# VectorE and ScalarE in written order behind the output products, weights split five units ahead

## The chip, the cores and the metric

The kernel runs on one core of one Trainium2 chip. The metric is device microseconds (us) of one execution; the time of a kernel is the median of its runs. About 0.2% (some 5 us) is what a measurement of this kernel can tell from no change.

## What is computed

Two stacks in a chain, for 256 positions and width 1024, all in fp32: two hybrid layers (retention, gated linear attention and forgetting attention side by side, then a convolved gated feed-forward part), and four layers with one mixer each (mLSTM, sliding window, HGRN2, differential attention) and a SwiGLU part. Every norm is modulated by columns that come from a product of a conditioning vector with large matrices ("ada"). Cut to what matters here:

```python
def hybrid_layer(...):                      # twice
    mod = c_act @ w_ada + b_ada
    h = modulate(rms_norm(x, norm1_g), shift1, scale1)
    ...                                     # three branches of h @ w_in
    mixed = jnp.sum(gates * y_br, axis=2) @ w_o
    x = x + gate1 * mixed
    h2 = modulate(rms_norm(x, norm2_g), shift2, scale2)
    u, g = jnp.split(h2 @ w_up, 2, axis=-1)
    u = causal_dwconv(u, w_conv, b_conv)    # three taps
    x = x + gate2 * ((jax.nn.silu(u) * g) @ w_down)

def layer(x, mixer):                        # four times: DeepNorm form
    ...                                     # x = layer_norm(ALPHA * x + (1 + gate) * mixer(modulate(x)))
def swiglu(h, w_in, w_out):
    gu = h @ w_in
    return (jax.nn.silu(gu[..., :FFN_HIDDEN]) * gu[..., FFN_HIDDEN:]) @ w_out
```

## The kernel before

**Products.** Each fp32 product is made of split parts: a weight and an activation are each held as a high part and a low rest, and a 128x128 block costs three matmuls (high by high, high by low, low by high; L497 to L499 where the output has features on partitions). Weights come in **units** of 128x1024, 689 of them, that is eight blocks. `load_unit` fetches a unit by DMA, casts it to the high part on ScalarE (the **cast**, tile h, L465) and subtracts on VectorE (the **low**, tile l, L466); `blocks` calls it when a unit's first block is about to be used. The h and l buffers are five deep each (pool ph). A product tile gathers eight blocks (22 in the products named down and fo) into one of four PSUM buffers (dps). In the transposed products the first four tiles that follow a norm run as one group on the unnormed activations (the early tiles, y, L765 and L766), and the norm's factors are applied behind it (fix, L777 to L781); four more tiles (mps) run on the normed ones, and single tiles follow.

**Stages.** By name: wo, up and down are the output product and the feed-forward part of the two hybrid layers; ml_w, sw_w, hg_w and df_w are the output products of the four mixers, fi and fo their feed-forward parts, and sw_in, hg_*, df_* the first products of the next mixers. At the end of an output product the residual tiles Z0 to Z7 (or X0 to X7) are formed; sums of their squares go through TensorE (stat), a chain of small VectorE instructions on 128x2 tiles makes the inverse root (`moments`, L721 to L734, with L671 to L679 in `rsqrt_short`), TensorE spreads it over the partitions (L743), ScalarE copies that (L746), and the tiles follow (L1380 to L1389).

**In the hybrid feed-forward part** tiles come in pairs: the even one gets its first tap on ScalarE (Identity, L859 from dps), two taps on VectorE (L1243, L1245) and silu (L859 from t); the odd one multiplies (L1251), and the product is split (L486 on ScalarE, L487 on VectorE). SwiGLU has silu, product and split alone.

**The order.** The program is written down instruction by instruction, and a scheduler then decides the order on every engine from its own costs; only pieces under `issue_after` are tied to others. The ada pieces (288 of 512 KB, one VectorE sum each, L415) are put in by `pump` at rates per stage (RATES): so many a product tile.

## Time and profile before

| | |
|---|---|
| median of 3 runs | 2322.12 us (2321.53 to 2323.61) |
| the profiled execution: its own time | 2321.35 us |
| its span in the trace | 2319.0 us |
| TensorE busy / weight loads | 2203.2 / 2115.6 us |
| VectorE busy | 1819.6 us |
| ScalarE busy | 1264.3 us |
| GpSimd busy | 106.8 us |
| mean granted TensorE clock | 0.979 of full speed |

TensorE is busy in 95% of the span. What is left is some 116 us at which it stands still, the start and the tail among them. Starts of the stages that the text speaks of, in us: up0 301 to 428, down0 to 491, the second hybrid layer's mixer to 751, wo1 to 774, up1 to 901, down1 to 965, ml_w 1067 to 1091, fi0 1091, sw_in 1295, sw_w 1348, fi1 1392, fo1 1531, hg 1596 to 1764, fi2 1764, df 1965 to 2103, fi3 2103, fo3 2240.

### The profile page before, as it was taken

Reading aid. Unit: us, or ns where it says so; the run is one execution under the profiler, and the core shown is the slowest. Engines: PE = TensorE matmul, PEld = TensorE weight load, DVE = VectorE, ACT = ScalarE, POOL = GpSimd, SP = SyncE. Lnnn points to the kernel's source line nnn. Section 1 sums busy time; section 2 is a strip of 40 time slices with the busy share of each in tenths; the row PEclk is TensorE's granted clock in tenths of the full one; section 3 lists DMA queues with packets and bytes.
Section 4 is the critical chain, followed back from the end, with each engine's and each line's share of the span. In section 5 each row is a group of like instructions: output and inputs, shape, how many; then the busy total and the mean of one; then the engine's idle time right before and its main releaser. Section 6 shows DMA issues by size and latency. Waiting matters only on the chain.

```text
span 2319.0 us, 46070 instructions
## 1 busy us (share of the span) xinstructions
PE 2203.2 (95%) x18071; PEld 2115.6 (91%) x18071; DVE 1819.6 (78%) x3465; ACT 1264.3 (55%) x2452; POOL 106.8 (5%) x280
## 2 busy tenths in 40 slices
PE   6999999999999999989899998999988999988997
PEld 5899999997999999979899888999878999878997
DVE  8879897988778878947878868688668778968655
ACT  3545465555454654545644676445755544766543
POOL 0011000002010000021000000000010000030000
PEclk9999999999999999989999998999998999999999
DMA  9659756978677568935789426787444788434751
GB/s 368 241 184 356 261 193 220 360 254 281 229 268 240 173 227 283 380 128 181 246 272 312 144 92 199 229 286 240 156 151 150 237 266 288 164 119 147 244 182 37
DMA packets 144938, 521.14 MB, mean 225 GB/s; under 512 B 16208, under 2 KB 18512, under 8 KB 144720
## 3 DMA queue, kind: packets, MB, share of 16 engines
q1 hardware_dynamic: 144432, 518.03, 65.5%
q8 instruction: 141, 2.31, 0.4%
q14 instruction: 77, 0.63, 0.1%
q10 hardware_dynamic: 288, 0.16, 0.0%
HBM read 517.08 MB, written 1.05 MB: 223 GB/s over the span
## 4 chain that ended last, share of the span: by engine, by line
PE 42%; issue 26%; DVE 3%; ACT 3%; POOL 2%; DMA 1%; ACTq 0%; POOLq 0%; DVEq 0%
PE dps L497 12%; PE dps L498 12%; PE dps L499 11%; POOL nr L634 1%; PE dps L506 1%; PE dps L505 1%; PE dps L504 1%; ACT t L859 1%; ACT h L465 1%; DVE l L466 1%; DMA w<-in_ada_dram 1%; PE mps L497 0%; PE mps L498 0%; PE mps L499 0%; PE mps L1674 0%
## 5 line engine op out<-in xcount | busy, mean ns | idle before, releaser
L497 PE MATMUL dps<-t,h 128*128 128x256 f32 (+1 forms) x4776 | 1358.3, 285 | 1.5 <-ACT t L791 0.7
L498 PE MATMUL dps<-t,h 128*128 128x256 f32 (+1 forms) x4776 | 1349.8, 283 | 2.3 <-DVE t L487 1.3
L499 PE MATMUL dps<-t,l 128*128 128x256 f32 (+1 forms) x4776 | 1347.2, 282 | 1.7 <-DVE l L466 1.7
L465 ACT CAST h<-w 128x1024 fp32r<-128x1024 f32 x689 | 719.8, 1052 | 539.0 <-PE dps L498 281.8
L466 DVE TENSOR_TENSOR l<-w,h 128x1024 fp32r<-128x1024 f32 x689 | 838.4, 1221 | 211.3 <-ACT h L465 208.4
L497 PEld LDWEIGHTS dps<-t,h 128*128 128x128 f32 x4776 | 904.6, 190 | 6.4 <-issue 1.9
L499 PEld LDWEIGHTS dps<-t,l 128*128 128x128 f32 x4776 | 905.6, 190 | 4.0 <-DVE l L466 2.1
L498 PEld LDWEIGHTS dps<-t,h 128*128 128x128 f32 x4776 | 904.2, 189 | 4.9 <-DVE t L487 2.3
L415 DVE SCALAR_TENSOR_TENSOR junk<-w,cb 128x1024 bf16<-128x1024 f32 x288 | 351.6, 1221 | 97.1 <-DMA w<-in_ada_dram 90.6
L486 ACT CAST t<-t 128x256 fp32r<-128x256 f32 x172 | 69.3, 406 | 125.8 <-DVE t L1419 75.6
L504 PE MATMUL dps<-h,t 128*128 128x512 f32 (+1 forms) x288 | 105.2, 374 | 8.3 <-ACT t L1388 6.3
L505 PE MATMUL dps<-l,t 128*128 128x512 f32 (+1 forms) x288 | 105.8, 371 | 1.6 <-DVE l L466 1.6
L506 PE MATMUL dps<-h,t 128*128 128x512 f32 (+1 forms) x288 | 104.3, 371 | 0.0
L816 POOL TENSOR_SCALAR nr<-nr 128x2 f32<-128x2 f32 (+2 forms) x22 | 13.3, 606 | 1592.5 <-ACT junk L859 1562.4
L487 DVE TENSOR_TENSOR t<-t,t 128x256 fp32r<-128x256 f32 x172 | 71.1, 419 | 8.7 <-ACT t L486 8.7
L504 PEld LDWEIGHTS dps<-h,t 128*128 128x128 f32 x288 | 56.3, 196 | 17.6 <-ACT t L1388 7.1
L765 ACT ACTIVATE t<-Z,c 128x256 fp32r<-128x256 f32 x56 | 28.5, 508 | 74.9 <-DVE Z L1364 74.9
L505 PEld LDWEIGHTS dps<-l,t 128*128 128x128 f32 x288 | 56.4, 196 | 10.8 <-DVE l L466 2.8
L506 PEld LDWEIGHTS dps<-h,t 128*128 128x128 f32 x288 | 55.8, 196 | 8.1 <-DVE t L1389 0.2
L497 PE MATMUL mps<-t,h 128*128 128x256 f32 x192 | 47.6, 308 | 15.1 <-ACT t L1388 13.6
L498 PE MATMUL mps<-t,h 128*128 128x256 f32 x192 | 55.0, 298 | 0.1
L499 PE MATMUL mps<-t,l 128*128 128x256 f32 x192 | 54.3, 295 | 0.0
(383 smaller groups left out, 2021.1 us busy)
## 6 DMA issues: line engine op xcount, KB each, us to landing
w<-in_w_dram SPq DMA_DIRECT2D x689, 512.0 KB, 4.5
w<-in_ada_dram SPq DMA_DIRECT2D x288, 512.0 KB, 5.1
t<-in_c_dram SPq DMA_DIRECT2D x4, 256.0 KB, 4.2
X<-in_x_dram SPq DMA_DIRECT2D x8, 128.0 KB, 3.8
v<-in_ret_dram SPq DMA_DIRECT2D x2, 512.0 KB, 9.0
out_dram<-X SPq DMA_DIRECT2D x8, 128.0 KB, 2.0
cols<-in_cols_dram SPq DMA_DIRECT2D x1, 737.0 KB, 6.8
const<-in_const_dram SPq DMA_DIRECT2D x1, 387.0 KB, 7.8
```

The source lines that it names most:

```text
L415: self.nc.vector.scalar_tensor_tensor(out=self.junk, in0=w, scalar=0.5, in1=self.cb, op0=ALU.mult, op1=ALU.mult, accum_out=self.mod[l][:, ...
L465: nc.scalar.copy(h[:, q:e], raw[:, q:e]).ins,
L466: nc.vector.tensor_tensor(out=low[:, q:e], in0=raw[:, q:e], in1=h[:, q:e].bitcast(F32), op=ALU.subtract).ins]
L486: nc.scalar.copy(t[:, 0], src)
L487: nc.vector.tensor_tensor(out=t[:, 1], in0=src, in1=t[:, 0].bitcast(F32), op=ALU.subtract)
L497: mm(pt, lhsT=h, rhs=x[:, 0], start=first, stop=False)
L498: mm(pt, lhsT=h, rhs=x[:, 1], start=False, stop=False)
L499: self.last_mm = mm(pt, lhsT=low, rhs=x[:, 0], start=False, stop=last).ins
L504: mm(pt, lhsT=x[:, 0, sl], rhs=h, start=first, stop=False)
L505: mm(pt, lhsT=x[:, 0, sl], rhs=low, start=False, stop=False)
L506: self.last_mm = mm(pt, lhsT=x[:, 1, sl], rhs=h, start=False, stop=last).ins
L765: self.nc.scalar.activation(out=h, in_=z, func=AF.Copy, scale=a)
```

## The change

From wo0 on to the end of down1, and from ml_w on to the end of the program, VectorE and ScalarE get a hand-written order (`manual_schedule`): their instructions stand in the order in which the program writes them. TensorE, GpSimd and the DMA queue are still ordered by the scheduler. Nothing closes the order at the next first products: `free_order` is called at the end of down1 and at the end, and the flag `ending` is set but read nowhere. So the second hybrid layer's mixer and the mixers swa, hgrn and diff are inside.

Inside it, `blocks` issues the split of unit u+5 at the first block of unit u; h and l get six buffers. The low half of an activation's split is held until the next weight unit has been split (or another point of release). A product tile's ada pieces are handed out block by block, and the rates change. `residual` loses its tie to the last tile. Counts of instructions stay the same, but for one table load less on ScalarE. Line numbers of the new kernel: cast L472, low L473, ada L422, activation split L521 and L522, Identity and silu L903, taps L1288 and L1290, product L1296, residual L1392 and L1412, early L806 to L808, moments L762 to L775 with L711 to L719, spread L784 and copy L787, fix L820 to L824, tile L1428 to L1438.

```diff
-RATES = dict(... up=0.1, down=3, fi=0.2, fo=2.5, ... fi0=0.5, ...)
+RATES = dict(... up=0.3, down=1.5, fi=0.36, fo=1.5, ... fi0=0.6, ...)
-        self.ph = ctx.enter_context(tc.tile_pool(name="ph", bufs=5))
+        self.ph = ctx.enter_context(tc.tile_pool(name="ph", bufs=6))
...
     def blocks(self, n):
-        if self.cunit is None or self.cunit[0] != u:
-            self.cunit = (u, self.load_unit(u * UNIT))
+        while max(self.ready, default=-1) < min(u + self.ahead, len(self.units) - 1):
+            i = max(self.ready, default=-1) + 1
+            self.ready[i] = self.load_unit(*self.units[i])
+            self.release()
+    def hold(self, piece):
+        if self.order is None:
+            piece()
+        else:
+            self.held.append(piece)
+    def ordered(self):
+        if self.order is None:
+            self.order = ExitStack()
+            self.order.enter_context(self.tc.manual_schedule(engines={mybir.EngineType.DVE, mybir.EngineType.Activation}))
+            self.ahead = AHEAD
...
         if scale is None:
             nc.scalar.copy(t[:, 0], src)
-            nc.vector.tensor_tensor(out=t[:, 1], in0=src, in1=t[:, 0].bitcast(F32), op=ALU.subtract)
+            self.hold(lambda: nc.vector.tensor_tensor(out=t[:, 1], in0=src, in1=t[:, 0].bitcast(F32), op=ALU.subtract))
...
+            if self.order is not None:
+                self.pump(pump / kt)
-        self.pump(pump)
+        if self.order is None:
+            self.pump(pump)
...
+        self.ordered()
         n2 = self.rms_begin(l, 3, "n2")
...
+        if last:
+            self.free_order()
+        self.ending = True
...
+            self.ordered()
             hx = self.residual_norm(("ml_w", "sw_w", "hg_w", "df_w")[i], ys, i, 0, None if last else nxt)
```

**VectorE in the product up0, before.** Two pairs of tiles; l is the low of a weight unit, the tiles t with numbers are activations.

```order
L466 TENSOR_TENSOR l<-w,h 128x1024
L1243 SCALAR_TENSOR_TENSOR t_4253<-dps,cols,t_4253 128x255
L1245 SCALAR_TENSOR_TENSOR t_4253<-dps,cols,t_4253 128x254
L466 TENSOR_TENSOR l<-w,h 128x1024
L1251 TENSOR_TENSOR t_4253<-t_4253,dps 128x256
L487 TENSOR_TENSOR t_4290<-t_4253,t_4290 128x256
L466 TENSOR_TENSOR l<-w,h 128x1024
L1243 SCALAR_TENSOR_TENSOR t_4324<-dps,cols,t_4324 128x255
```

**The same place after.**

```order
L1296 TENSOR_TENSOR t_4578<-t_4578,dps 128x256
L473 TENSOR_TENSOR l<-w,h 128x1024
L522 TENSOR_TENSOR t_4618<-t_4578,t_4618 128x256
L1288 SCALAR_TENSOR_TENSOR t_4652<-dps,cols,t_4652 128x255
L1290 SCALAR_TENSOR_TENSOR t_4652<-dps,cols,t_4652 128x254
L473 TENSOR_TENSOR l<-w,h 128x1024
L1296 TENSOR_TENSOR t_4652<-t_4652,dps 128x256
```

The low half of the product's split (L522) now stands behind the next unit's low, and ahead of the taps.

**ScalarE in up0, before.** L859 from dps is the first tap, L859 from t the silu.

```order
L465 CAST h<-w 128x1024
L859 ACTIVATE t_4253<-dps,cols 128x256
L465 CAST h<-w 128x1024
L859 ACTIVATE t_4253<-t_4253 128x256
L486 CAST t_4290<-t_4253 128x256
L465 CAST h<-w 128x1024
```

**The same place after.**

```order
L472 CAST h<-w 128x1024
L903 ACTIVATE t_4288<-dps,cols 128x256
L903 ACTIVATE t_4288<-t_4288 128x256
L472 CAST h<-w 128x1024
L521 CAST t_4325<-t_4288 128x256
L472 CAST h<-w 128x1024
```

The second cast of a pair stood ahead of the silu and stands behind it now.

**VectorE at the start of fi1, before:** the end of the chain of small instructions (nr) and the first instructions behind the spread (L778 on).

```order
L466 TENSOR_TENSOR l<-w,h 128x1024
L673 TENSOR_TENSOR nr<-nr 128x2
L415 SCALAR_TENSOR_TENSOR junk,mod_128<-w,cb 128x1024
L674 TENSOR_TENSOR nr<-nr 128x2
L466 TENSOR_TENSOR l<-w,h 128x1024
L675 SCALAR_TENSOR_TENSOR nr<-nr 128x2
L415 SCALAR_TENSOR_TENSOR junk,mod_128<-w,cb 128x1024
L676 SCALAR_TENSOR_TENSOR nr<-nr 128x2
L677 TENSOR_TENSOR nr<-nr 128x2
L678 SCALAR_TENSOR_TENSOR nr<-nr 128x2
L679 SCALAR_TENSOR_TENSOR nr<-nr 128x2
L734 TENSOR_TENSOR nr<-nr 128x2
```

**The same place after.**

```order
L714 TENSOR_TENSOR nr<-nr 128x2
L715 SCALAR_TENSOR_TENSOR nr<-nr 128x2
L716 SCALAR_TENSOR_TENSOR nr<-nr 128x2
L717 TENSOR_TENSOR nr<-nr 128x2
L718 SCALAR_TENSOR_TENSOR nr<-nr 128x2
L719 SCALAR_TENSOR_TENSOR nr<-nr 128x2
L775 TENSOR_TENSOR nr<-nr 128x2
L473 TENSOR_TENSOR l<-w,h 128x1024 x3
L821 TENSOR_TENSOR t_17249<-dps,t_17210 128x256
```

The chain now stands in one piece, and three lows of weight units stand between it and the first fix (L821).

**VectorE at the end of the output product sw_w, before:** the last residual tiles (Z_120 and Z_121 are Z6 and Z7).

```order
L1344 SCALAR_TENSOR_TENSOR Z_118<-dps,mod_127,X_90 128x256
L1344 SCALAR_TENSOR_TENSOR Z_119<-dps,mod_127,X_91 128x256
L1364 TENSOR_TENSOR Z_118<-Z_118,t_16792 128x256
L1364 TENSOR_TENSOR Z_119<-Z_119,t_16792 128x256
L713 TENSOR_TENSOR t_16791<-t_16791,Z_118 128x256
L766 SCALAR_TENSOR_TENSOR t_16990<-Z_118,c_16777,t_16990 128x256
```

**The same place after.**

```order
L1392 SCALAR_TENSOR_TENSOR Z_118<-dps,mod_127,X_90 128x256
L1412 TENSOR_TENSOR Z_118<-Z_118,t_16764 128x256
L749 TENSOR_TENSOR t_16763<-t_16763,Z_118 128x256
L808 SCALAR_TENSOR_TENSOR t_16965<-Z_118,c_16749,t_16965 128x256
L752 TENSOR_TENSOR t_16762<-t_16762,t_16968 128x256
L473 TENSOR_TENSOR l<-w,h 128x1024
L1392 SCALAR_TENSOR_TENSOR Z_119<-dps,mod_127,X_91 128x256
```

Two residual tiles ran interleaved; now one tile is finished, with a weight unit's low behind it, before the next begins.

## Rows read from the trace of the kernel before

**Rows 1.** The page, busy time of each engine.

```profile
PE 2203.2 (95%) x18071; PEld 2115.6 (91%) x18071; DVE 1819.6 (78%) x3465; ACT 1264.3 (55%) x2452; POOL 106.8 (5%) x280
```

**Rows 2.** Groups by line, up0's steady stretch (317 to 428.4): count, busy us, mean ns, idle before.

```profile
L466 DVE TENSOR_TENSOR l<-w,h 128x1024 fp32r<-128x1024 f32 x39 | 47.6, 1219 | 6.7 <-ACT h L465 6.7
L415 DVE SCALAR_TENSOR_TENSOR junk<-w,cb 128x1024 bf16<-128x1024 f32 x12 | 14.6, 1219 | 4.0 <-DMA w<-in_ada_dram 4.0
```

**Rows 3.** Timeline of VectorE in up0: start, length (us), line, idle before and releaser.

```profile
360.92 0.48 DVE L1243 SCALAR_TENSOR_TENSOR t<-dps,cols,t 128x255 f32<-128x255 f32 x1
361.43 0.48 DVE L1245 SCALAR_TENSOR_TENSOR t<-dps,cols,t 128x254 f32<-128x254 f32 x1
361.83 1.22 DVE L466 TENSOR_TENSOR l<-w,h 128x1024 fp32r<-128x1024 f32 x1
362.96 0.42 DVE L1251 TENSOR_TENSOR t<-t,dps 128x256 f32<-128x256 f32 x1
363.85 0.42 DVE L487 TENSOR_TENSOR t<-t,t 128x256 fp32r<-128x256 f32 x1 [0.47 <-ACT t L486]
364.80 1.23 DVE L466 TENSOR_TENSOR l<-w,h 128x1024 fp32r<-128x1024 f32 x1 [0.53 <-ACT h L465]
365.95 0.48 DVE L1243 SCALAR_TENSOR_TENSOR t<-dps,cols,t 128x255 f32<-128x255 f32 x1
```

**Rows 4.** Timeline of ScalarE in the same stretch.

```profile
360.56 1.06 ACT L465 CAST h<-w 128x1024 fp32r<-128x1024 f32 x1 [0.36 <-PE dps L498]
362.01 0.42 ACT L859 ACTIVATE t<-t 128x256 f32<-128x256 f32 x1 [0.39 <-DVE t L1245]
363.41 0.41 ACT L486 CAST t<-t 128x256 fp32r<-128x256 f32 x1 [0.99 <-DVE t L1251]
363.73 1.05 ACT L465 CAST h<-w 128x1024 fp32r<-128x1024 f32 x1
```

**Rows 5.** Windows: stretch, length, busy PE, PEld, DVE, ACT, POOL, granted clock, DMA share, GB/s.

```profile
317.00:428.40 111.40, 111.40 (x949) 111.36 (x947) 96.49 (x166) 68.25 (x112) 0.00 (x0) 1.00 0.68 231
428.40:490.70 62.30, 62.30 (x531) 62.30 (x531) 58.84 (x92) 29.87 (x46) 0.00 (x0) 1.00 0.98 374
1423.00:1531.40 108.40, 108.40 (x922) 108.31 (x920) 76.40 (x121) 59.65 (x96) 0.00 (x0) 1.00 0.72 233
490.70:751.00 260.30, 254.99 (x1886) 236.98 (x1884) 206.35 (x365) 132.91 (x247) 26.85 (x48) 0.99 0.71 243
1295.10:1391.90 96.80, 94.52 (x700) 81.33 (x699) 71.85 (x223) 73.05 (x204) 0.00 (x0) 0.96 0.26 83
1596.20:1764.30 168.10, 152.56 (x1834) 137.74 (x1833) 126.65 (x269) 108.11 (x302) 14.76 (x48) 0.98 0.47 152
1964.90:2102.70 137.80, 124.17 (x978) 116.09 (x977) 107.80 (x290) 94.08 (x247) 27.58 (x96) 0.94 0.41 135
1391.90:1423.00 31.10, 22.78 (x160) 22.27 (x159) 24.49 (x60) 13.62 (x27) 0.00 (x0) 0.78 0.60 203
2067.90:2080.00 12.10, 9.30 (x75) 8.62 (x73) 3.78 (x5) 7.88 (x27) 8.30 (x33) 1.00 0.49 163
```

**Rows 6.** Timeline from sw_w's end (1391.9) to the restart in fi1, cut.

```profile
1393.82 0.48 DVE L1344 SCALAR_TENSOR_TENSOR Z<-dps,mod,X 128x256 f32<-128x256 f32 x1
1395.34 0.42 DVE L1364 TENSOR_TENSOR Z<-Z,t 128x256 f32<-128x256 f32 x1
...
1409.92 2.08 PE L743 MATMUL mps<-const,nr 128*128 128x128 f32 x8 [4.92 <-DVE nr L679]
1412.03 0.59 ACT L746 COPY t<-mps 128x512 f32<-128x512 f32 x1 [5.97 <-PE mps L743]
1412.65 0.42 DVE L778 TENSOR_TENSOR t<-dps,t 128x256 f32<-128x256 f32 x1 [2.59 <-ACT t L746]
...
1415.39 1.01 PE L497 MATMUL mps<-t,h 128*128 128x256 f32 x3 [3.40 <-ACT t L1388]
```

**Rows 7.** Groups by line, whole span: the spread's matmuls on TensorE, with their waits.

```profile
L743 PE MATMUL mps<-const,nr 128*128 128x128 f32 x80 | 15.0, 340 | 22.3 <-DVE nr L679 18.9 <-DVE nr L664 3.3
```

More of the change, by code (lines that the diff above doesn't have):

```diff
@@ L28 @@
 LATE = True
+AHEAD = 5
 SUMS, KNOWN = 5, 21
@@ L189, in pack_ada @@
     return out
-RATES = dict(rv0=0, rk0=0, rq0=0.05, gk0=0, gg0=1, rg0=2, mg0=0.75, up=0.1, down=3, fi=0.2, fo=2.5, wo=0.0, ml_w=0.0,
+RATES = dict(rv0=0, rk0=0, rq0=0.05, gk0=0, gg0=1, rg0=2, mg0=0.75, up=0.3, down=1.5, fi=0.36, fo=1.5, wo=0.0, ml_w=0.0,
              sw_w=0.0, hg_w=0.0, df_w=0.0, br=1.0, sw_in=0.0, df_kq=0.0, df_v0=2.0, df_v1=0.0, hg_v=1.5, ml_v=3.0,
-             fq=3.0, fk=3.0, fv=3.0, gv=3.0, rv=3.0, gk=1.5, hg_qf1=0.2, s1=1.25, fi0=0.5, hg_g=0.6, ml_o=0.6,
+             fq=3.0, fk=3.0, fv=3.0, gv=3.0, rv=3.0, gk=1.5, hg_qf1=0.2, s1=1.25, fi0=0.6, hg_g=0.6, ml_o=0.6,
              gv1=1.25, fv1=4, wo0=0.1, df_kq1=0.1, ml_v1=4)
@@ L310, in __init__ @@
         self.specs, _ = dense_specs()
+        self.units, self.ready, self.ahead, self.order = [], {}, 0, None
+        for s in self.specs:
+            s["first"] = len(self.units)
+            self.units += [(s, lo) for lo in range(0, s["cols"], UNIT)]
         self.si = 0
+        self.held = []
+        self.ending = False
         self.bg = list(range(len(ADA_ORDER)))
@@ L449, in begin, with load_unit @@
         self.si += 1
-        self.cur, self.cpos, self.cunit = s, 0, None
+        self.cur, self.cpos = s, 0
         return s
-    def load_unit(self, lo):
-        nc, s = self.nc, self.cur
+    def load_unit(self, s, lo):
+        nc = self.nc
         hi = min(s["cols"], lo + UNIT)
@@ L470, in blocks @@
     def blocks(self, n):
-        pos = self.cpos
-        u, r = divmod(pos, UNIT)
-        if self.cunit is None or self.cunit[0] != u:
-            self.cunit = (u, self.load_unit(u * UNIT))
-        h, low = self.cunit[1]
+        u, r = divmod(self.cpos, UNIT)
+        u += self.cur["first"]
+        while max(self.ready, default=-1) < min(u + self.ahead, len(self.units) - 1):
+            i = max(self.ready, default=-1) + 1
+            self.ready[i] = self.load_unit(*self.units[i])
+            self.release()
+        for i in [i for i in self.ready if i < u and i + 8 < max(self.ready)]:
+            del self.ready[i]
+        h, low = self.ready[u]
         assert r + n <= UNIT
@@ L479, in blocks, with release, free_order @@
         return h[:, r:r + n], low[:, r:r + n]
+    def hold(self, piece):
[3 more added lines that the diff above has]
+            self.held.append(piece)
+    def release(self):
+        while self.held:
+            self.held.pop(0)()
+    def ordered(self):
[3 more added lines that the diff above has]
+            self.ahead = AHEAD
+    def free_order(self):
+        if self.order is not None:
+            self.release()
+            self.order.close()
+            self.order, self.ahead = None, 0
     def split(self, src, scale=None):
@@ L547, in dense_tile @@
                 self.step(self.mid)
-        self.pump(pump)
+            if self.order is not None:
+                self.pump(pump / kt)
+        if self.order is None:
+            self.pump(pump)
         return pt
@@ L589, in dense_T @@
                 norm["later"].pop(0)()
+        self.release()
         return xs
@@ L707, in stat @@
         self.act(out=two(sq), in_=z, func=AF.Square)
+        if f and sums["centred"]:
+            nc.vector.tensor_tensor(out=two(acc[1]), in0=sums["first"] if f == 1 else two(acc[1]), in1=z, op=ALU.add)
+        self.release()
         if f:
@@ L711, in stat @@
             sums["first"] = z
-        if f and sums["centred"]:
-            nc.vector.tensor_tensor(out=two(acc[1]), in0=sums["first"] if f == 1 else two(acc[1]), in1=z, op=ALU.add)
     def moments(self, st, centred, eps):
@@ L765, in early @@
         self.nc.scalar.activation(out=h, in_=z, func=AF.Copy, scale=a)
-        self.nc.vector.scalar_tensor_tensor(out=low, in0=z, scalar=a, in1=h.bitcast(F32),
-                                            op0=ALU.mult, op1=ALU.subtract)
         self.nc.scalar.copy(y[:, :, S:S + 2], ab[:, :, f, :])
+        self.hold(lambda: self.nc.vector.scalar_tensor_tensor(
+            out=low, in0=z, scalar=a, in1=h.bitcast(F32), op0=ALU.mult, op1=ALU.subtract))
+        if f == 7:
+            self.release()
         return y
@@ L790, in modulated @@
         t = self.t2([128, 2, S], F32R)
+        self.release()
         nc.scalar.activation(out=t[:, 0], in_=u, func=AF.Identity, bias=B[:, f:f + 1])
-        nc.vector.scalar_tensor_tensor(out=t[:, 1], in0=u, scalar=B[:, f:f + 1], in1=t[:, 0].bitcast(F32),
-                                       op0=ALU.add, op1=ALU.subtract)
+        self.hold(lambda: nc.vector.scalar_tensor_tensor(
+            out=t[:, 1], in0=u, scalar=B[:, f:f + 1], in1=t[:, 0].bitcast(F32), op0=ALU.add, op1=ALU.subtract))
         return t
@@ L1386, in tile @@
             u = self.t1()
+            self.release()
             self.act(out=two(u), in_=z[f], func=AF.Identity, scale=cA[:, f:f + 1], bias=cB[:, f:f + 1])
-            ready[0] = nc.scalar.copy(t[:, 0], u).ins
-            nc.vector.tensor_tensor(out=t[:, 1], in0=u, in1=t[:, 0].bitcast(F32), op=ALU.subtract)
+            nc.scalar.copy(t[:, 0], u)
+            self.hold(lambda: nc.vector.tensor_tensor(out=t[:, 1], in0=u, in1=t[:, 0].bitcast(F32), op=ALU.subtract))
             return t
-        ready = {}
         def residual(f):
-            with self.tc.issue_after(ready[0]):
+            if True:
                 self.act(out=two(self.X[f]), in_=z[f], func=AF.Identity, scale=aG[:, f:f + 1], bias=aB[:, f:f + 1])
@@ L2028, in finish @@
     def finish(self):
+        self.free_order()
         for f in range(8):
```

4 lines of the change are left out of this document (3 added, 1 removed).

## The prediction, made before the changed kernel was run

> **What bounds the kernel now.** I read the busy times first [rows 1]: TensorE 2203.2 of 2319.0 us, so it is the bound and can give back 116 us at the most. VectorE at 78% and ScalarE at 55% look free, but these are means over stages. I took the stretches next [rows 5]. In up0 VectorE is busy 96.49 of 111.40 us and ScalarE 68.25, TensorE all of it at full clock: VectorE and ScalarE together have 164.7 us of work in 111.4, so 53 us of it must overlap, and the order decides whether it can. In fi1 the sum is 136.1 of 108.4. Then I went down to single instructions in up0 [rows 3, 4], to the start of fi1 [rows 6], and to the spread's waits over the whole span [rows 7].
>
> **The pair loop in up, the main term.** One pair of tiles is a loop through both engines, since each instruction hands on to the next. Before, from start to start [rows 3, 4]: product L1251 at 362.96, activation cast 363.41 (0.45), weight cast 363.73 (0.32), low 364.80 (1.07), first tap 365.95 (1.15), second tap (0.51, from 360.92 to 361.43), low (0.40), product (1.13, 361.83 to 362.96). That sums to 5.03, which is the distance of the two first taps shown, 360.92 and 365.95. TensorE needs longer: 39 units in 111.40 us [rows 2, 5], 2.86 a tile, 5.71 a pair. So the loop hides, with 0.7 us to spare, and ada sums fit in here and there.
>
> Three things get into that loop by the new order. The held low half (L522) comes between the low and the taps: one 0.42 instruction [rows 3], about 0.38 back to back. The second weight cast stands behind the silu, so the second tap must end, the silu run and the cast follow: 0.58 (361.43 to 362.01) for silu to begin, 0.32 until the cast can (as for the activation cast, 363.41 to 363.73), then 1.07 to the low and 1.13 to the product, where before the low followed the tap after 0.40 because its cast was done. The new loop: 0.45 + 0.32 + 1.07 + 1.13 + 0.38 + 0.51 + 0.58 + 0.32 + 1.07 + 1.13 = 6.96 us. The Identity is hidden beside the low. The split ahead doesn't help: it moves which unit is cast, not where in the queue the cast stands.
>
> Single tiles in up are 36 of 44, or 18 pairs: 18 x (6.96 - 5.71) = 22.5 us. Up to ten ada sums in up0 and nine in up1 now stand between a low and the next evacuation, on the loop, at 1.14 to 1.22 each [rows 2]: about 11 us. Of these 33.5 the four PSUM buffers let TensorE run ahead by up to three tiles, 8.6 us, but what isn't lost there is partly lost at down's first tile, which needs the last hidden tile near its end; I take off 8. So **+26 a time, +52 for up0 and up1**. Ends for both together: +20 if the ada sums find holes and the buffers and down's slack absorb more than half of the rest, +67 if nothing is absorbed.
>
> **The start of a feed-forward part.** In fi1 before, the last residual tile is finished at 1395.76, 3.9 us behind sw_w's end, the spread begins at 1409.92, and the normed product restarts at 1415.39, 23.5 us behind [rows 6]. The chain of small instructions in between has weight lows and ada sums in every joint. After, it runs in one piece: some 14 instructions of about 0.2, so 3 us. Against that, the residual tiles come later. One written tile is residual and shift (0.8 us together, as two instructions like those of rows 3), early cast and square on ScalarE (0.9 with the hand-over), weight cast 1.05, low 1.14: about 4.0 a tile for tiles 4 to 7, where TensorE needs 2.86, and about 2.2 each for tiles 0 to 3. From the group's end, 12.4 us ahead of the stage's end, that is 8.8 + 1.2 + 3 x 4.0 + 0.9 = 22.9, so Z7 is done 10.5 us behind the end, 6.6 later than now. Sum and chain give the spread at some 15.5 (now 18.0). Then the three lows: the third waits for a cast that stands behind the spread's copy, so 2.7 us to the copy's end, 1.05 and 1.22, and from there 2.7 to the restart as now (1412.65 to 1415.39): 23 to 26. Over fi0 to fi3 I take +2 each, **+8**, ends -20 and +30. For the two ups, whose start is short now, the written tile loop costs some 5 each, **+11** with the clock behind it, ends 0 and +20.
>
> **The mixers.** They fall under the written order too. The sum of both engines beyond the stretch's length, which would be the loss if nothing overlapped [rows 5]: second hybrid mixer 206.35 + 132.91 - 260.3 = 79, sliding window 48, HGRN2 67, differential 64, together 258. Between these ends two rows have a worked loop: in up 33.5 of 53 come out, six tenths; in fi the loop without taps is product, activation cast, weight cast, silu, weight cast, low, 0.45 + 0.32 + 0.96 + 0.35 + 1.07 + 1.13 = 4.3, or 5.4 with an ada sum, under 5.71, so none of 28 does. The mixers have several heads side by side, but rotary chains and exponentials are written head by head; they are nearer to fi in load and to up in the length of a chain. I take 15%, **+40**, ends 0 and +130.
>
> **Edits with one answer.** down and fo have fewer ada sums: VectorE is at 58.84 of 62.30 in down0 and TensorE has no gap there [rows 5], so at most a microsecond or two in fo: **-4**. fi's own steady part: 0. One table load less, the sixth buffer and the released `residual`: 0, as TensorE waits for none of them.
>
> **Sum**, against the profiled execution's own 2321.35: +52 + 8 + 11 + 40 - 4 = +107, so 2428.4; the median is 0.8 higher, so **2429**. All low ends together give 2318, all high ends 2565; half-way to each, since they won't all fall together, 2374 to 2497.
>
> **Rivals.**
> 1. *Faster: the chain in one piece wins.* TensorE waits 18.9 us for the chain at six norms [rows 7], and behind such a wait the granted clock is low: 0.78 over the first 31.1 us of fi1, with 22.78 busy [rows 5]. If up's loop hid (the lead of five units and the buffers swallowing it) and the residual tiles kept TensorE's pace, the 18.9 would go, and about half as much again at the clock: 2321 - 30 = 2290. It decides at the written tile loop being under 2.86 and the pair loop under 5.71. Against it: the sums above, worked out from distances seen between the same instructions. Chance 0.20, of which 0.03 end within 0.2%.
> 2. *The up loop hides, the rest stays:* an order of instructions that overlaps better than I read, or slack in the buffers. Then 2429 - 52, with a few us, 2380. Chance 0.11.
> 3. *The mixers serialise as much as up does,* half of their 258: 2429 + 90 = 2520. For it: VectorE and ScalarE take turns on each item. Against it: several heads in flight. Chance 0.10.
> 4. *TensorE's clock falls in up.* In the slow stretch TensorE would wait about 1.3 to 1.9 us in each pair. In 2067.9 to 2080 it was busy 9.30 of 12.1 us, with waits of 1 to 2 us, and the clock stayed at 1.00 [rows 5]; so I expect full clock at a share of 5.71 in 7.6. [...] Chance 0.05.
> That the change doesn't do what its few words say is so in one point already: the written order doesn't end at the next first products, which is in the mixers' term. If it were closed there, that term would go and the time be 2389, still slower.
>
> **How the numbers follow.** The forecast has 0.54, and the rivals 0.20, 0.11, 0.10 and 0.05. Predicted is the forecast's 2429. Its own range, 2374 to 2497, holds rivals 2 and 4 too; to leave out no more than 2 in 10 I go down to 2300, into the upper part of rival 1, and up to 2530 for rival 3. Within 0.2% is about what a measurement of this kernel can tell from no change. Faster by more: 0.17, from rival 1. Within: 0.03. Slower: the forecast and rivals 2 to 4, 0.80.
>
> **What would show it.** In up0 after: the product L1296 every 7.0 us, 7.6 where an ada sum stands in between, with TensorE waiting for VectorE on a PSUM buffer, up0 at about 150 us in place of 127, VectorE's share of it lower, and the lows waiting for casts. In fi1: the spread about 15 us behind the output product's end and the restart at 23 to 26; L743's waits shorter, the group's matmuls waiting for the last early tiles instead. In sliding window, HGRN2 and differential attention some 5 to 15 us more each, with TensorE waiting on both engines in turn. I would be wrong in the main term if the pair distance in up stays under 5.75, in the boundaries if the restart comes before 20, in the mixers if their stretches don't grow.

## The result, and the profile after

The changed kernel takes 2603.46 us (2601.61 to 2606.02) beside 2322.83: a ratio of 1.121, interval 1.119 to 1.123. It is slower, as forecast, but by 281 us and not by 107, and lies above the range that was given (2300 to 2530).

The busy times of the page after, to be laid beside [rows 1]:

```profile
PE 2292.1 (88%) x18071; PEld 2168.1 (83%) x18071; DVE 1860.8 (72%) x3465; ACT 1260.4 (48%) x2451; POOL 107.3 (4%) x280
```

The same work in a longer span: VectorE's share falls from 78 to 72%, ScalarE's from 55 to 48%, TensorE's from 95 to 88%; the engines wait for each other. TensorE's busy time grew as well, by 89 us for the same number of matmuls, at a mean granted clock of 0.946 (before 0.979). The spans are 2319.0 and 2599.8 us. By stage, from a stage's first matmul to the next one's, in us ("mixer" with the output product behind it, and the second hybrid mixer without wo1):

```
                     before   after   forecast     closed   closed, silu, old rates
up0 + up1             253.8   337.0     +63         336.8     274.4
second hybrid mixer   260.3   292.0  )              272.4     273.6
sliding window         96.8   138.4  )  +40          98.5     104.1
HGRN2                 168.1   200.5  )  in all      179.5     176.8
differential          137.7   199.5  )              164.5     145.5
fi0 to fi3            553.2   573.7     +8          574.7     573.5
down and fo           399.0   405.9     -4          407.0     402.1
```

A forecast of +63 is the prediction's +52 and +11. "Closed" is the run with the order closed at the next first products, and the last column takes two more causes away; both are below. The up products lost 83 us (63 forecast with their starts), the four mixers 168 (40 forecast), fi0 to fi3 21 (8 forecast, for their starts). The stretches of after that answer to [rows 5] (a part of up0, the second hybrid mixer, sliding window, HGRN2, differential; columns as there):

```profile
349.00:400.00 51.00, 42.45 (x333) 40.65 (x332) 31.59 (x49) 21.20 (x34) 0.00 (x0) 0.98 0.53 176
533.10:825.10 292.00, 264.25 (x1885) 241.49 (x1884) 208.99 (x359) 129.85 (x249) 28.18 (x48) 0.98 0.65 222
1417.80:1556.20 138.40, 105.75 (x699) 86.80 (x698) 77.12 (x221) 71.38 (x197) 0.00 (x0) 0.80 0.22 73
1764.80:1965.30 200.50, 162.79 (x1833) 145.06 (x1832) 133.25 (x272) 106.98 (x294) 13.00 (x48) 0.91 0.42 141
2178.50:2377.90 199.40, 145.46 (x977) 131.00 (x976) 126.47 (x309) 94.26 (x245) 28.06 (x96) 0.83 0.36 125
```

In sliding window VectorE's and ScalarE's busy times add up to 148.5 of 138.4 us: only ten of them had to overlap (before 144.9 in 96.8, so 48). In the two traces the engines were busy together for 29 us, and for 55 before. In this part of up0 TensorE, busy all the time before, now stands still for 17%.

**The pair loop in up0.** VectorE in the steady part, one pair and an ada sum, then ScalarE in the second half of it (timeline: start, length, instruction, idle before it):

```profile
373.55 0.41 DVE L1296 TENSOR_TENSOR t<-t,dps 128x256 f32<-128x256 f32 x1
375.39 1.23 DVE L473 TENSOR_TENSOR l<-w,h 128x1024 fp32r<-128x1024 f32 x1 [1.43 <-ACT h L472]
376.54 0.42 DVE L522 TENSOR_TENSOR t<-t,t 128x256 fp32r<-128x256 f32 x1
376.87 1.22 DVE L422 SCALAR_TENSOR_TENSOR junk<-w,cb 128x1024 bf16<-128x1024 f32 x1
378.01 0.08 DVE L422 DVE_READ_ACCUMULATOR junk<-w,cb 128x1 f32 x1
378.01 0.48 DVE L1288 SCALAR_TENSOR_TENSOR t<-dps,cols,t 128x255 f32<-128x255 f32 x1
378.53 0.48 DVE L1290 SCALAR_TENSOR_TENSOR t<-dps,cols,t 128x254 f32<-128x254 f32 x1
380.49 1.23 DVE L473 TENSOR_TENSOR l<-w,h 128x1024 fp32r<-128x1024 f32 x1 [1.48 <-ACT h L472]
381.63 0.41 DVE L1296 TENSOR_TENSOR t<-t,dps 128x256 f32<-128x256 f32 x1
```

```profile
379.10 0.42 ACT L903 ACTIVATE t<-t 128x256 f32<-128x256 f32 x1 [3.28 <-DVE t L1290]
379.43 1.03 ACT L472 CAST h<-w 128x1024 fp32r<-128x1024 f32 x1
382.08 0.41 ACT L521 CAST t<-t 128x256 fp32r<-128x256 f32 x1 [1.62 <-DVE t L1296]
```

From product to product it is 8.08 us with the ada sum (373.55 to 381.63) and 6.94 without (seven places beside nine of the other), where 6.96 was forecast without one. With one, the prediction's sum and its 1.14 for the ada sum give 8.1, and the 7.6 among its signs was too short. Each engine's idle time names the other as its releaser: ScalarE waits 3.28 us for the taps, VectorE 1.48 for the cast behind the silu.

**The start of fi1**, to be laid beside [rows 6] (sw_w ends at 1556.2):

```profile
1567.97 0.42 DVE L1412 TENSOR_TENSOR Z<-Z,t 128x256 f32<-128x256 f32 x1
...
1573.88 1.16 PE L784 MATMUL mps<-const,nr 128*128 128x128 f32 x8 [1.01 <-DVE nr L719]
1575.07 0.59 ACT L787 COPY t<-mps 128x512 f32<-128x512 f32 x1 [3.19 <-PE mps L784]
...
1576.64 1.23 DVE L473 TENSOR_TENSOR l<-w,h 128x1024 fp32r<-128x1024 f32 x1 [0.34 <-ACT h L472]
1577.78 0.42 DVE L821 TENSOR_TENSOR t<-dps,t 128x256 f32<-128x256 f32 x1
...
1580.64 0.58 PE L532 MATMUL mps<-t,h 128*128 128x256 f32 x1 [5.60 <-ACT t L1437]
```

Z7 is done 12.2 us behind the end of sw_w (3.9 before, 10.5 forecast), the spread begins at 17.7 (18.0; 15.5) and the restart is at 24.4 (23.5; 23 to 26). The wait ahead of the spread is down to 1.0 us from 4.9, and the one behind it up to 5.6 from 3.4: the third low (1576.64) stands between the copy and the fix.

### The profile page after: what moved, and what is told of

It reads as the page before. It is cut to its first block, busy times and chain, and to the rows that moved or that the text cites. A ratio compares the mean times of both kernels' runs of the same rounds, so it can differ in the third digit from the quotient of the medians.

```text
span 2599.8 us, 46146 instructions
## 1 busy us (share of the span) xinstructions
PE 2292.1 (88%) x18071; PEld 2168.1 (83%) x18071; DVE 1860.8 (72%) x3465; ACT 1260.4 (48%) x2451; POOL 107.3 (4%) x280
## 4 chain that ended last, share of the span: by engine, by line
PE 42%; issue 22%; DVE 21%; ACT 12%; POOL 2%; DMA 2%; SPq 0%; DVEq 0%; ACTq 0%; POOLq 0%
PE dps L532 11%; PE dps L533 11%; PE dps L534 11%; DVE l L473 7%; ACT h L472 6%; DVE junk L422 4%; ACT t L903 3%; PE dps L539 1%; PE dps L541 1%; PE dps L540 1%; DVE t L522 1%; POOL nr L674 1%; DVE t L1290 1%; DMA w<-in_w_dram 1%; DVE Z L1429 1%
## 5 line engine op out<-in xcount | busy, mean ns | idle before, releaser
L532 PE MATMUL dps<-t,h 128*128 128x256 f32 (+1 forms) x4776 | 1380.9, 290 | 110.8 <-DVE t L1290 39.0
L533 PE MATMUL dps<-t,h 128*128 128x256 f32 (+1 forms) x4776 | 1362.3, 286 | 4.4 <-DVE t L522 3.8
L534 PE MATMUL dps<-t,l 128*128 128x256 f32 (+1 forms) x4776 | 1360.0, 285 | 5.4 <-DVE l L473 5.4
L473 DVE TENSOR_TENSOR l<-w,h 128x1024 fp32r<-128x1024 f32 x689 | 833.8, 1221 | 477.0 <-ACT h L472 463.4
L532 PEld LDWEIGHTS dps<-t,h 128*128 128x128 f32 x4776 | 917.8, 193 | 138.1 <-issue 71.1
L533 PEld LDWEIGHTS dps<-t,h 128*128 128x128 f32 x4776 | 919.9, 193 | 7.8 <-DVE t L522 4.5
L534 PEld LDWEIGHTS dps<-t,l 128*128 128x128 f32 x4776 | 919.3, 193 | 8.2 <-DVE l L473 6.9
L472 ACT CAST h<-w 128x1024 fp32r<-128x1024 f32 x689 | 708.4, 1047 | 198.0 <-PE dps L533 97.9
L422 DVE SCALAR_TENSOR_TENSOR junk<-w,cb 128x1024 bf16<-128x1024 f32 x288 | 350.9, 1218 | 12.1 <-ACT junk L903 8.1
L521 ACT CAST t<-t 128x256 fp32r<-128x256 f32 x172 | 70.1, 408 | 358.0 <-DVE t L1466 208.2
L806 ACT ACTIVATE t<-Z,c 128x256 fp32r<-128x256 f32 x56 | 28.7, 513 | 136.2 <-DVE Z L1412 136.2
L539 PEld LDWEIGHTS dps<-h,t 128*128 128x128 f32 x288 | 58.8, 205 | 28.7 <-ACT t L1437 8.7
L532 PE MATMUL mps<-t,h 128*128 128x256 f32 x192 | 54.8, 312 | 30.3 <-ACT t L1437 22.4
L903 ACT ACTIVATE t<-t 128x256 f32<-128x256 f32 (+1 forms) x65 | 27.1, 419 | 98.5 <-DVE t L1290 98.3
L522 DVE TENSOR_TENSOR t<-t,t 128x256 fp32r<-128x256 f32 x172 | 70.4, 418 | 2.8 <-ACT t L521 2.8
L903 ACT ACTIVATE t<-mps,nr 128x128 f32<-128x128 f32 x64 | 26.2, 427 | 92.0 <-DVE nr L1979 41.6
L532 PEld LDWEIGHTS mps<-t,h 128*128 128x128 f32 x192 | 39.3, 217 | 31.4 <-ACT t L1437 23.2
```

The costliest lines, as they stand in the source:

```text
L422: self.nc.vector.scalar_tensor_tensor(out=self.junk, in0=w, scalar=0.5, in1=self.cb, op0=ALU.mult, op1=ALU.mult, accum_out=self.mod[l][:, ...
L472: nc.scalar.copy(h[:, q:e], raw[:, q:e]).ins,
L473: nc.vector.tensor_tensor(out=low[:, q:e], in0=raw[:, q:e], in1=h[:, q:e].bitcast(F32), op=ALU.subtract).ins]
L521: nc.scalar.copy(t[:, 0], src)
L522: self.hold(lambda: nc.vector.tensor_tensor(out=t[:, 1], in0=src, in1=t[:, 0].bitcast(F32), op=ALU.subtract))
L532: mm(pt, lhsT=h, rhs=x[:, 0], start=first, stop=False)
```

## The experiments

### The order closed at the next first products

```diff
-        if last:
-            self.free_order()
+        self.free_order()
...
-            self.ending = True
+            self.free_order()
```

> The changed kernel, but the written order is closed at the next first products: after down0 and down1, and after each fo. If the written order inside the mixers costs their +167 us (second hybrid mixer +32, sliding window +42, HGRN2 +32, differential +62), these stretches go back to their lengths of before within some 5 us each and the time falls from 2603 to about 2436. If the loss there came from the splits ahead, the sixth buffer or the rates, which stay, it would remain above 2560. up0 and up1 should stay at 168 us each under both.

2483.06 us, ratio 1.069 (1.067 to 1.071): 120 us come back, and not 167, 115 of them in the mixers. Sliding window is back at 98.5, but df_w stays at 52.5 us (before 34.7), hg_w at 32.1 (26.6), df_kq0 at 25.8 (18.2) and hg_qf0 at 21.8 (17.2), and in the second hybrid mixer rk1 and gg1 together are 10 us longer than before. df_w's start in this kernel, VectorE and TensorE's longest wait:

```profile
2234.13 0.17 DVE L448 SCALAR_TENSOR_TENSOR mod<-mod,cols 128x8 f32<-128x8 f32 x1
...
2235.28 8.04 DVE L473 TENSOR_TENSOR l<-w,h 128x1024 fp32r<-128x1024 f32 x7
```

```profile
PE dps L534 <- DVE l L473: 9.7, 1, 9.7
```

Ahead of it VectorE runs eight ada sums from 2215 on, the last five in a row, since the residual's gate (L448) needs them all; the lows come after, and TensorE waits 9.7 us for one. So closing the order in the mixers gives back 115 us, and the other 52 have another cause. Closing also ends the split ahead and the holding there (`free_order` sets the lead to 0), which the expectation counted among what stays. The two runs below that change these under the written order speak against them as the cause: the four mixers take 830 us in the changed kernel, 843 with a lead of three units, and 854 without the holding.

### The silu behind the second cast

```diff
-                self.act(out=u, in_=u, func=AF.Silu)
+                self.hold(lambda: self.act(out=u, in_=u, func=AF.Silu))
```

> The changed kernel, with one thing moved: in up the silu of the even tile is held until the odd tile's weight unit has been cast, so the cast no longer stands behind it. If the pair loop through both engines sets up's pace (6.95 us a pair seen, 8.08 with an ada sum), the loop becomes 0.45 + 0.32 + 1.07 + 1.13 + 0.38 + 0.51 + 0.40 + 1.13 = 5.4 us, under TensorE's 5.71, and 6.5 where an ada sum stands in it: up0 and up1 about 135 us each in place of 168, the time about 2537. If PSUM buffers or the late start set the pace, under 20 us are gained.

In this kernel the silu of the first eight tiles of up falls behind their product, so that part of the values differs; the instructions are the same. 2547.50 us: 56 us less, 67 expected. VectorE, and ScalarE beside it, in up0:

```profile
378.72 0.42 DVE L1296 TENSOR_TENSOR t<-t,dps 128x256 f32<-128x256 f32 x1
380.56 1.23 DVE L473 TENSOR_TENSOR l<-w,h 128x1024 fp32r<-128x1024 f32 x1 [1.42 <-ACT h L472]
...
382.55 0.48 DVE L1290 SCALAR_TENSOR_TENSOR t<-dps,cols,t 128x254 f32<-128x254 f32 x1
382.95 1.22 DVE L473 TENSOR_TENSOR l<-w,h 128x1024 fp32r<-128x1024 f32 x1
384.08 0.41 DVE L1296 TENSOR_TENSOR t<-t,dps 128x256 f32<-128x256 f32 x1
```

```profile
380.89 1.03 ACT L472 CAST h<-w 128x1024 fp32r<-128x1024 f32 x1
383.12 0.42 ACT L903 ACTIVATE t<-t 128x256 f32<-128x256 f32 x1 [1.20 <-DVE t L1290]
```

The distance is 5.36 (378.72 to 384.08) and 6.50 with an ada sum, as worked out, and the second low follows the tap with no idle time. The loop is the cause of up's pace. up0 is 141.2 us and not 135: its start doesn't come back (TensorE still waits 3.9 us ahead of the normed tiles), and behind 350 TensorE stands still for 4 us more, since 6.50, the distance with an ada sum, is above its 5.71.

### The hybrid layers left to the scheduler

```diff
-        self.ordered()
         n2 = self.rms_begin(l, 3, "n2")
```

> The changed kernel, with the two hybrid layers left to the scheduler: the written order begins at ml_w only. If the stages' losses add up, up0 and up1 give back 83 us, the second hybrid mixer 32 and wo0 1: about 2487. If part of the loss in the later layers came from what the hybrid layers leave behind (ada pieces put off, units out of step), the later stages move by more than 5 us.

2509.66 us, 94 less, for 2487 expected. up0 and up1 are 129.5 and 129.7, the second mixer 263.1 (before 260.3), but down0 and down1 69 us each (62 and 64 before): under the scheduler the new rates cost some 10 us there (in the first chain run below, which leaves these layers to the scheduler at the rates of before, they are 62.6 and 63.2). The mixers of the second stack stay within 3 us of the changed kernel's, so no more than that is handed on from the hybrid layers to them.

### The ada rates of before

```diff
-RATES = dict(... up=0.3, down=1.5, fi=0.36, fo=1.5, ... fi0=0.6, ...)
+RATES = dict(... up=0.1, down=3, fi=0.2, fo=2.5, ... fi0=0.5, ...)
```

> The changed kernel with the ada rates of before. Even with the order closed in the mixers, df_w was 53 us (before 35), hg_w 32 (27) and fo2 72 (63), with a run of ada sums and weight lows ahead of the residual in df_w. If that is ada work put off by the new rates, df_w, hg_w and fo2 give back some 30 us together, and up0 and up1, whose rate falls from 0.3 to 0.1 a tile, some 8 us each, as the loop's long distance of 8.08 becomes rarer: 2603 to about 2557. If the rates don't matter there, the time stays within 10 us of 2603.

2593.15 us: 10 less, not 46. fo2 is back (63.0) and df_w partly (42.3), up0 and up1 give 8 each as expected, but down0 grows from 62.7 to 75.1 and the second hybrid mixer by 9, rk1 alone by 11. down0 has 25 ada sums there and rk1 six, where the changed kernel has 12 and one. Ada work taken out of one stage is met again in another that is no less full; the expectation counted only the gains.

### Three causes taken away together

The three edits above, and in up:

```diff
                 u = keep[0]
+                self.release()
                 nc.vector.tensor_tensor(out=u, in0=u, in1=pt, op=ALU.mult)
```

> Three of the suspected causes taken away together from the changed kernel: order closed at the next first products, silu behind the second cast in up (released ahead of each product), ada rates of before. If they are the causes and add up: 2603 - 120 - 55 - about 45 = about 2383, with some 40 of the 60 us left over before in the starts of up and fi and the written tile loops of wo and the mixers' output products. If they overlap, it stays above 2410.

2402.12 us, ratio 1.035 (1.033 to 1.036), for 2383 expected. df_w, hg_w and fo2 are at their lengths of before (34.2, 27.1, 62.8), and the pair distance in up0 is 5.36 at most places, under TensorE's 5.71. What is left, 80 us, lies mostly in stages' starts: up0 and up1 +10 each, fi0 to fi3 +20 together, rk1 +12, hg_qf0 and df_kq0 +7 to +8 each, sw_in +6. down0 has +7, and not at its start: TensorE is busy throughout its first 10.8 us and stands still for 4 us after that. No run took these apart further.

### The oldest stage first

An attention item has four stages or more, and each step issues one stage of several items, the newest item's scores first. The edit in `push`, and the same in `tail`:

```diff
-        self.fill += [self.items[n - 1 - j][j] for j in range(n) if j < len(self.items[n - 1 - j])]
+        self.fill += [self.items[n - 1 - j][j] for j in reversed(range(n)) if j < len(self.items[n - 1 - j])]
```

> The changed kernel, with the stages of an attention item written the other way round: at each step the oldest item's last stage first, the newest item's scores last (sliding window, differential attention, and mLSTM, which is outside of the written order). If the loss in the mixers is that in written order the newest item's scores, which wait for TensorE, stand ahead of older items' work that is ready, the distance of items in the sliding window falls from 13.4 to 9 or 10 us, sliding window from 138 to about 105 and differential from 199 to about 165: 2603 to about 2530. If the weight casts in the queue or the clock are the cause, it stays within 20 us of 2603.

2582.87 us, 21 less, and 10 of those in mLSTM, which isn't under the written order. Sliding window falls from 138.4 to 130.1, differential with df_w from 199.5 to 195.6: the expectation was far off, and the run comes out near its other case (within 20 us of 2603), with the weight casts in the queue or the clock as the cause. An item in the changed kernel shows what stands in line (ScalarE and then VectorE, one item of 13.4 us; then the window of that item, columns as in [rows 5]):

```profile
1486.21 0.37 ACT L903 ACTIVATE t<-mps,nr 128x128 f32<-128x128 f32 x1 [7.23 <-DVE nr L1728]
...
1487.92 1.50 ACT L903 ACTIVATE t<-t,nr 128x128 f32<-128x128 f32 x4
1489.30 0.86 ACT L1756 COPY t<-mps 128x384 f32<-128x384 f32 x2
1490.03 0.40 ACT L521 CAST t<-mps 128x256 fp32r<-128x256 f32 x1
1490.30 0.64 ACT L903 ACTIVATE X<-Z,c 128x256 f32<-128x256 f32 x1
1490.80 1.07 ACT L472 CAST h<-w 128x1024 fp32r<-128x1024 f32 x1
```

```profile
1491.90 1.22 DVE L473 TENSOR_TENSOR l<-w,h 128x1024 fp32r<-128x1024 f32 x1 [5.24 <-ACT h L472]
1493.05 0.42 DVE L522 TENSOR_TENSOR t<-mps,t 128x256 fp32r<-128x256 f32 x1
...
1494.50 0.43 DVE L1687 TENSOR_TENSOR t<-t,t 128x256 f32<-128x256 f32 x1
1498.27 1.15 DVE L1726 TENSOR_REDUCE nr<-mps 128x1 f32<-128x128 f32 x4 [3.34 <-PE mps L1721]
```

```profile
1486.21:1499.65 13.44, 8.35 (x39) 6.04 (x39) 4.71 (x16) 5.66 (x19) 0.00 (x0) 0.57 0.12 40
```

Exponentials, older items' weights and copies, cast, low, rotary chain, TensorE's scores, maximum, and exponentials again (1499.65): one line through three engines. Their busy times in it add up to 18.7 us in 13.44, so on the average 1.4 of the three are busy. The weight cast is one link of that line, and so is a slower TensorE: the granted clock is 0.57 there, and a matmul of L534 at 1494.43 takes 0.41 us, where in up0 at a clock of 1.00 these take 0.28. Oldest first takes only the older items' weights and copies off it (1.50 and 0.86 us), and the distances go to 9.4 to 12.2.

### The scores one step later

```diff
-                self.push(lambda: scores(t, q, pp), lambda: weights(pp), ...)
+                self.push(lambda: None, lambda: scores(t, q, pp), lambda: weights(pp), ...)
...
-                    self.step(4)
+                    self.step(5)
```

On top of oldest first, in the sliding window alone.

> The changed kernel with stages oldest first, and in the sliding window the scores one step later, so that an item's scores no longer stand behind its own rotary chain and the product tile in the same step. If an item's line through the engines (rotary on VectorE, scores on TensorE, maximum on VectorE, exponentials on ScalarE, then the next unit's cast and low) is what spaces items at 13.4 us in the changed kernel and 9.4 to 12.2 with oldest first, taking TensorE's scores off it brings the distance to 8 to 9 and sliding window from 130 us to 115 or less; 2583 to about 2568. If the written order as such costs the time, whatever the line, sliding window stays at 130.

2572.88 us. The reciprocals of one item and the next (VectorE's timeline) now stand 7.7 apart, 7.7 to 9.0 over the stretch:

```profile
1451.66 0.18 DVE L1744 RECIPROCAL nr<-nr 128x4 f32<-128x4 f32 x1
1459.38 0.18 DVE L1744 RECIPROCAL nr<-nr 128x4 f32<-128x4 f32 x1
1467.10 0.18 DVE L1744 RECIPROCAL nr<-nr 128x4 f32<-128x4 f32 x1
```

Sliding window is 120.4 us for 115 expected. The two edits give back 18 of its 42 us with the order still written out: this part of the cost belongs to the line that this order makes, and not to a written order as such. Of the other 24 no run shows whether a better written order would give them back. The granted clock in sliding window rose with it, to 0.89 from 0.80 (0.87 with oldest first alone), so what part of the 18 is the line and what the clock behind it isn't shown either.

### Three units ahead in place of five

```diff
-AHEAD = 5
+AHEAD = 3
```

> The changed kernel with weights split three units ahead in place of five. The forecast held that the lead changes which unit is cast and not where the cast stands in the queue, so that it neither helps nor costs: within 10 us of 2603. If the lead of five hides part of the loops' pace (rival: buffers swallow it), three units lose up to 2 x 2.86 us of it in each of some ten stages, 20 to 50 us slower.

2637.42 us, 34 more: in the range of the expectation's rival (20 to 50 slower), though not in up. The pair distances in up0 are the same to 0.01 us (6.94 and 8.08), so on up's loop the lead does nothing, as the prediction said; but down0 and down1 lose 4 us each, fi1 to fi3 2 to 5, HGRN2 with its output product 9 and sw_in 11, while sw_w is 9 shorter. The lead is worth something outside of up; by what, no run shows.

### Without the holding

```diff
     def hold(self, piece):
-        if self.order is None:
-            piece()
-        else:
-            self.held.append(piece)
+        piece()
```

> The changed kernel without the holding: the low half of an activation's split is written right behind its high half, not behind the next weight unit's low. In up it then runs while ScalarE casts the weight unit, and leaves the pair loop: 6.95 - 0.38 = 6.57 us a pair, and 8.08 becomes 7.7, so up0 and up1 are 7 us shorter each. At the tiles behind a norm, VectorE waits for ScalarE's cast some 0.4 us a tile in its place. In sum 2603 to about 2590; 2603 or more if the holding is worth what it was put in for, elsewhere.

2632.63 us, 29 more, where 2590 was expected. The distances in up0 are 6.60 and 7.74, just as worked out, but up0 gains only 2.7 us, and most other places lose: fi0 to fi3 3 to 8 us each, sw_in 5, HGRN2's first products 5 and hg_w 5. The held low is on the loop in up, and holding is worth more than that elsewhere.

### Only the chain, and only where it gains

Two runs look for rival 1's gain. In the first the order is opened at the sums of a start in the second stack and closed behind the first four fixed tiles, three units ahead, rates of before (`fetch` is the loop of `blocks` that splits ahead).

```diff
-        self.ordered()
         n2 = self.rms_begin(l, 3, "n2")
...
-            self.ordered()
             hx = self.residual_norm(...)
...
         def sums():
+            if nxt:
+                self.ordered()
+                self.fetch(self.cur["first"])
             self.stat(st, 7, self.Z[7])
...
                 self.release()
+                self.free_order()
```

> The written order only where rival 1 had its gain: opened at the sums of a feed-forward or mixer start in the second stack and closed behind the first four fixed tiles, three units ahead there, all else to the scheduler, rates of before. The residual tiles of the output product then keep their interleaved order. If the chain in one piece is worth what TensorE waits for it (18.9 us at six norms, five of which are in this kernel's stretches) and the clock behind it, 2322 falls to about 2300 to 2312. If the wait only moves on to the fix, as in the changed kernel's fi1 (4.9 and 3.4 us before, 1.2 and 5.6 after), it stays within 5 us of 2322.

2343.34 us, ratio 1.010 (1.008 to 1.012): slower than before. The waits of the spread and of the normed product over the whole span, to be laid beside [rows 7], in this kernel:

```profile
L789 PE MATMUL mps<-const,nr 128*128 128x128 f32 x80 | 12.8, 304 | 6.5 <-DVE nr L709 3.3 <-DVE nr L724 3.1
L536 PE MATMUL mps<-t,h 128*128 128x256 f32 x192 | 47.1, 304 | 20.8 <-ACT t L1444 19.6 <-ACT t L840 1.3
```

The wait for the chain falls from 18.9 to 3.1 us, and the normed product's rises from 15.1 to 20.8:

```profile
L497 PE MATMUL mps<-t,h 128*128 128x256 f32 x192 | 47.6, 308 | 15.1 <-ACT t L1388 13.6 <-ACT t L791 1.4
```

That last line is from the kernel before. fi1 to fi3 are 2 to 3 us shorter each, but sw_in, HGRN2's and differential's starts and fo0 to fo2 lose 2 to 8 each. The second run keeps the order at fi1 to fi3 alone, and writes the stages oldest first in mLSTM alone.

```diff
-            if nxt:
+            if nxt and s == 0 and i:
                 self.ordered()
...
         def known():
+            self.ahead = min(self.ahead, 2)
...
+        self.oldest = True
         self.dense_T("ml_qk", hx, evac_qk)
```

> What gained in the two runs before, alone: the written order only from the sums to the fixed tiles at the starts of fi1, fi2 and fi3 (each 2 to 3 us shorter there), with one split fewer between spread and fix, and the stages oldest first in mLSTM only (8 us shorter there); rates of before. The starts of the mixers, which lost 6 to 8 us each, are left to the scheduler. Expected 2320 - 8 - 8, and a few us for the split moved: about 2300 to 2306, faster than both kernels. If the gains depend on the rest, it stays within 5 us of 2320.

2310.79 us beside 2321.17 for before, ratio 0.9960 (0.9945 to 0.9974): a little faster than both kernels. In the profiled execution mLSTM is 9 us shorter, fi1 to fi3 6.9 together and sw_in 5; half of it is lost again around them, ml_w +1.4, fi0 +1.3, fo0 +3.1, HGRN2 +2. Oldest first throughout the kernel before, with nothing else (the edit shown above, in `push` and `tail`):

> The kernel before, with one edit: the stages of the attention items written oldest first. With it in the changed kernel the mLSTM part, which the scheduler orders there too, fell from 104 to 94 us. If the scheduler keeps that, the time is about 2312; if it makes the written order of the stages irrelevant, 2322 within 3.

2316.77 us beside 2319.89, ratio 0.9984 (0.9976 to 0.9993): mLSTM gains 8 and sw_w 3, sw_in, fo0 and ml_w lose 8. The gain is no larger than what such a measurement can tell.

## Why the prediction was wrong in size

The forecast missed by 174 us: 128 in the mixers, 20 in up, 13 in fi0 to fi3, 11 in down and fo, and a few elsewhere.

**The mixers: the step that failed and decided.** "I take 15%, +40" between ends of 0 and 130 was wrong; it was 168, beyond the upper end. The bound of 258 stood in the prediction, and 65% of it came, where the prediction had the 63% of up (33.5 of 53) in hand and set it aside because several heads are in flight. They are in flight in the program, but a step's stages were written so that each step is one line through the engines, as the item of sliding window shows. That the sum is so near to up's share is luck: by stretch it is 32 of 79 us (second hybrid mixer), 42 of 48 (sliding window), 32 of 67 (HGRN2) and 62 of 64 (differential). This is rival 3's mechanism, at more than its price and with a chance of only 0.10. 115 us of it go when the order is closed; of the other 52, 23 come from ada sums put off to the output products (df_w and hg_w, gone with the rates of before and the order closed), and gg1's 7 go with the same run; the rest lies mostly at starts, df_kq0 and hg_qf0 above all, where no run took it apart. Only sliding window's line was read from single instructions; that the other three lose by lines of the same kind is argued.

**The pair loop: right, its deduction not.** 6.96 us was forecast and 6.94 measured, with an ada sum 8.08 (8.1 by the sum, 7.6 among the signs), and the run with the silu moved gave 5.36 for a forecast of 5.4. Seven distances of 6.94 and nine of 8.08 are 30 us more than TensorE's 5.71 each. The step that failed here is "I take off 8" for what the four PSUM buffers let TensorE run ahead. That lead is used up by the first single tiles: the group's and the second four tiles' evacuations and a run of four casts have put VectorE behind already, and TensorE waits for it at 348.

```profile
347.98 0.55 PE L532 MATMUL dps<-t,h 128*128 128x256 f32 x1 [3.64 <-DVE t L1290]
```

With the start 4 us longer, up0 lost 41.4, where 33.5 for the loop, 5 for the start and no deduction give 38.5.

**The starts: right in kind.** Spread, third low and restart came at 17.7, 20.4 and 24.4 us for 15.5, 19.3 and 23 to 26; fi0 to fi3 lost 21, where 8 was taken and 30 was the end. Some 9 of the 21 are not at the starts: behind the first 31 us of these stages TensorE stands still for 9 us in all, 5 of them in fi0, where "fi's own steady part: 0" was forecast. Closing brings none of the 21 back, since the order is still open there. Rival 1 was right that the chain in one piece shortens its wait (18.9 to 7.4 us in the changed kernel), and wrong that the time goes with it: the normed product's wait behind it grew from 15.1 to 30.3, and the first of the two chain runs is slower than the kernel before.

**The rates: a sign missed.** "-4" for fewer ada sums in down and fo was +7 (fo2 alone +9). down0 and down1 do have fewer, 12 and 13 for 20 and 21, but fo2 has 22 for 12, put off to it by the lower rates; thirteen of them start between 2108 and 2125 us, and a cast waits 9.9 us there for the DMA of its weights, TensorE 6.7 for casts and lows. Before and after, in fo2, and that cast:

```profile
L415 DVE SCALAR_TENSOR_TENSOR junk<-w,cb 128x1024 bf16<-128x1024 f32 x12 | 14.6, 1220 | 5.3 <-DMA w<-in_ada_dram 5.3
L422 DVE SCALAR_TENSOR_TENSOR junk<-w,cb 128x1024 bf16<-128x1024 f32 x22 | 26.8, 1220 | 0.3
```

```profile
2120.44 1.05 ACT L472 CAST h<-w 128x1024 fp32r<-128x1024 f32 x1 [9.92 <-DMA w<-in_w_dram]
```

With the rates of before fo2 is back at 63.0. df_w's run of sums wasn't seen either: the order has eight ada sums there where there had been none, and the prediction only counted the stages from which they went.

**The clock in up: right, nearly.** At waits of one to two microseconds in each pair the granted clock was 1.00 of full speed from 350.9 to 456.7 us. It was 0.50 for 3.4 us three times: from 320.2 behind the 3.9 us wait at the start, from 347.5 in the wait of 3.6, and from 456.7 behind a wait of 2.1 like others that it had come through. So rival 4 isn't borne out by up's loop. What a lower clock over much of up would cost, for which the forecast's range makes room with rival 4, no run shows; what the trace shows is that TensorE began a matmul every 0.21 us in the last of the three stretches, and every 0.12 at 1.00. In sliding window and differential attention, where the mean is 0.80 and 0.83, the clock did go back and forth between 1.00 and 0.50 (in sliding window five stretches at 0.50, of 6.8 to 20.5 us, between 1436.3 and 1525.1); TensorE's longest waits there are 3.5 and 12.6 us.

**One line more in the change.** The changed kernel is also built with `dynamic_dma_scratch_size=1024`, which the description of the change doesn't name. This line and the sixth buffer reach the stages ahead of wo0 as well, where no order is written, and these take 255 us for 256 before.

## What to carry to other kernels

In a hand-written order follow one item's instructions from engine to engine and add up start-to-start distances seen in the old trace: if they come back to where they began, that sum is the pace, and here it was right to 0.03 us in three kernels (6.94, 5.36 and 6.60). Where no loop has been worked out, the busy time of the engines beyond the stretch is a bound that can come true: in the four mixers 40, 86, 49 and 96% of it came, in up's loop some 30 of 53 us, while in fi1's steady part TensorE stood still for 2 us where 28 was the bound. A share taken for all of them is a guess; follow one item in each. Before a steady loop is given slack from buffers, look at whether the stage's start has used it up, and when work is taken out of one stage, find the stage that meets it next.

## What was not expected of the hardware

TensorE's granted clock stayed up in one stretch full of waits and fell in another. Two windows of the changed kernel, up0's loop and a part of sliding window (columns as in [rows 5]):

```profile
350.90:456.70 105.80, 84.66 (x671) 80.56 (x671) 64.59 (x101) 44.56 (x70) 0.00 (x0) 1.00 0.54 180
1477.30:1497.80 20.50, 12.99 (x56) 8.88 (x58) 7.70 (x22) 7.34 (x21) 0.00 (x0) 0.50 0.16 52
```

In the first TensorE waited up to 2.1 us in every pair, and the clock stayed at 1.00 of full speed; in the second, with a wait of 1.3 us just ahead of it and three of 2.2 to 2.4 in it, it was at 0.50 throughout. A matmul of L534 (128x256) took 0.280 us on the average in the first and 0.415 in the second. In sliding window the clock adds to the loss: TensorE's own busy time there is 105.75 us, 94.5 before, for the same matmuls. What sets the two apart, no run shows.
